# A softmax over rows of 512: one load for the first tile, two blocks in the first tile, and a third row of five tiles scaled on ScalarE

## The chip, the cores and the metric

The kernel runs on one core of a Trainium2 chip. The metric is the device time of an execution in microseconds (us), here the median of several executions. The profile's clock starts a little later and ends a little earlier: the profiled execution of the kernel before took 162.04 us, its span is 160.3 us, and its last store landed at 159.4 on the span's clock. So I add 2.6 to 2.8 us to a landing to compare it with a time. A transfer is issued by an engine and carried by 16 DMA engines; it has landed when the last of the 16 reports its part done.

## The reference

```python
batch, seq, dim = 16, 1024, 512              # x is float32
x_scaled = x / 0.5
x_max = np.max(x_scaled, axis=-1, keepdims=True)
exp_x = np.exp(x_scaled - x_max)
return exp_x / np.sum(exp_x, axis=-1, keepdims=True)
```

That is 16,384 rows of 512: 33.55 MB in and 33.55 MB out.

## The kernel before

The rows are cut into 8 tiles of 128 partitions x 16 rows x 512, 4.19 MB each. A tile goes through these steps, in place: a load, issued by SyncE; the rows' maxima on VectorE (`shift`); the exponentials and their sums on ScalarE; the reciprocal and the scaling of most rows on VectorE; the scaling of the last rows on ScalarE; a store, issued by ScalarE. Six tiles are held at once in SBUF, the memory of the core (`BUFS = 6`), so the loads of tiles 0 to 5 are issued at once, and those of tiles 6 and 7 wait until the stores of tiles 0 and 1 have landed. A tile may be computed in blocks of rows; the first and the last are.

```python
    WHOLE = [(0, G)]                                            # G = 16
    LOADS = [[(0, 4), (4, G)]] + [WHOLE] * 7
    BLOCKS = [[(0, 4), (4, 8), (8, G)]] + [WHOLE] * 6 + [[(0, 8), (8, G)]]
    STORES = [WHOLE] * 8
    BUFS = 6
    # ... (cut: pools, a warm-up of the exponential, load(), shift(), exponentials())
    def scale_vector(i):
        c, lo, hi = blocks[i]
        b = hi - lo
        k = b - b // 8                                          # 14 of 16 rows, 7 of 8
        recips[i] = stats.tile([P, BMAX], fp32, name="recip")
        nc.vector.reciprocal(recips[i][:, 0:b], sums[i][:, 0:b])
        rows = chunks[c][:, lo : lo + k, :]
        nc.vector.tensor_mul(
            rows, rows, recips[i][:, 0:k].unsqueeze(2).broadcast_to((P, k, D))
        )

    def scale_scalar(i):
        c, lo, hi = blocks[i]
        b = hi - lo
        for g in range(b - b // 8, b):
            row = chunks[c][:, lo + g, :]
            nc.scalar.activation(
                out=row, in_=row, func=COPY, scale=recips[i][:, g : g + 1]
            )
    # ... (cut: store(), issued by ScalarE)
    for i in range(n):
        if i + 1 < n:
            exponentials(i + 1, rows(i + 1)[0])
        scale_vector(i)
        scale_scalar(i)
        if i + 2 < n:
            shift(i + 2)
        store(i)
        # ... (cut)
```

## Time and profile before

162.24 us, the median of 3 executions (162.10 to 162.29).

| what | value | where |
|---|---|---|
| VectorE busy | 134.6 us, 84% of the span | busy times |
| ScalarE busy | 102.2 us, 64% | busy times |
| 16 DMA engines busy | 97.9% | the two DMA queues, summed |
| rate of the DMA engines, stores alone | 434 GB/s | windows, 116 to 147.5 us |
| last store issued, landed | 147.5, 159.4 us | ScalarE's timeline, DMA issues |

A busy share tells how full an engine is, not whether the end hangs on it. Two of these resources are nearly full. The profile's chain of waits follows instructions back from the last one, and a transfer that is issued and then only has to finish is not in it.

### The profile page before, as it was taken

The numbers are of one execution on the slowest core, as the hardware profiler recorded it, in microseconds if no ns is written. First come the engines' busy times: TensorE is split into PE (matmuls) and PEld (weight loads), VectorE is DVE, ScalarE is ACT, GpSimd is POOL, SyncE is SP. The second block draws the span as 40 slices with busy tenths as digits, with TensorE's granted clock in tenths as the row PEclk, the third lists the DMA queues.
The fourth block names the chain that finished last, engine by engine and source line by source line (L and its number), as shares of the span: only waits on it lengthen the run. The fifth ranks groups of instructions, "written<-read, shape, count | busy, mean of one in ns | idle before, by whom it ended". The sixth has DMA issues, their size and how long they took to land.

```text
span 160.3 us, 402 instructions
## 1 busy us (share of the span) xinstructions
DVE 134.6 (84%) x45; ACT 102.2 (64%) x273; POOL 0.2 (0%) x4
## 2 busy tenths in 40 slices
DVE  0607999999999999999999999999999999957000
ACT  3071549069989972998199909991899891690000
POOL 0000000000000000000000000000000000000000
DMA  5999999999999999999999999999999999999993
GB/s 180 474 409 491 409 401 483 425 393 452 458 393 401 393 425 474 409 393 499 417 393 474 442 393 468 442 393 442 474 393 417 491 401 401 491 417 401 466 442 139
DMA packets 2450, 67.13 MB, mean 419 GB/s; under 512 B 272, under 2 KB 272, under 8 KB 272
## 3 DMA queue, kind: packets, MB, share of 16 engines
q1 hardware_dynamic: 1296, 33.56, 49.4%
q10 hardware_dynamic: 1152, 33.55, 48.5%
q14 instruction: 2, 0.02, 0.0%
HBM read 33.55 MB, written 33.55 MB: 419 GB/s over the span
## 4 chain that ended last, share of the span: by engine, by line
DVE 80%; DMA 7%; ACT 4%; issue 0%; SPq 0%
DVE negmax L74 42%; DVE xt L103 36%; DMA xt<-in_x_dram 7%; ACT xt L86 4%; DVE bias L78 1%; DVE recip L101 1%; SPq L66 0%
## 5 line engine op out<-in xcount | busy, mean ns | idle before, releaser
L86 ACT ACTIVATE xt<-xt,bias 128x512 f32<-128x512 f32 x128 | 90.4, 708 | 41.5 <-DVE bias L78 40.6
L74 DVE TENSOR_REDUCE negmax<-xt 128x16 f32<-128x8192 f32 (+2 forms) x11 | 69.9, 6353 | 9.5 <-DMA xt<-in_x_dram 9.5
L103 DVE TENSOR_TENSOR xt<-xt,recip 128x7168 f32<-128x7168 f32 (+2 forms) x11 | 62.0, 5637 | 0.4
L86 ACT ACTIVATION_READ_ACCUMULATOR xt<-xt,bias 128x1 f32 x128 | 23.9, 187 | 0.0
L112 ACT ACTIVATE xt<-xt,recip 128x512 f32<-128x512 f32 x15 | 9.9, 707 | 0.0
L101 DVE RECIPROCAL recip<-sums 128x16 f32<-128x16 f32 (+2 forms) x11 | 2.4, 218 | 1.8 <-ACT xt L86 1.8
L78 DVE TENSOR_SCALAR bias<-negmax 128x16 f32<-128x16 f32 (+2 forms) x11 | 1.9, 173 | 0.4
L52 ACT ACT_TABLE_LOAD x1 | 1.3, 1283 | 0.7 <-PEq L157 0.7
L51 DVE MEMSET warm<- 128x1 f32 x1 | 0.1, 59 | 0.8 <-PEq L157 0.8
L52 ACT ACTIVATE warm<-warm 128x1 f32<-128x1 f32 x1 | 0.2, 202 | 0.0
L157 POOL MEMSET const-bfloat16-1.0<- 128x1 bf16 x1 | 0.1, 101 | 0.0
L157 POOL MEMSET const-uint8-127<- 128x1 uint8 x1 | 0.1, 101 | 0.0
L157 POOL MEMSET const-float32-0.0<- 128x1 f32 x1 | 0.1, 98 | 0.2 <-issue 0.2
L157 POOL MEMSET const-float32-1.0<- 128x1 f32 x1 | 0.1, 98 | 0.0
## 6 DMA issues: line engine op xcount, KB each, us to landing
out_dram<-xt ACTq DMA_DIRECT2D x8, 4096.0 KB, 22.8
xt<-in_x_dram SPq DMA_DIRECT2D x7, 4096.0 KB, 30.1
xt<-in_x_dram SPq DMA_DIRECT2D x1, 3072.0 KB, 11.7
xt<-in_x_dram SPq DMA_DIRECT2D x1, 1024.0 KB, 4.8
```

What stands on the lines that cost most here:

```text
L51: nc.vector.memset(warm, 0.0)
L52: nc.scalar.activation(out=warm, in_=warm, func=EXP)
L74: nc.vector.tensor_reduce(negmax[:, 0:b], chunks[c][:, lo:hi, :], axis=AX, op=MAX, negate=True)
L78: nc.vector.tensor_scalar_mul(biases[i][:, 0:b], negmax[:, 0:b], 2.0)
L86: nc.scalar.activation(out=row, in_=row, func=EXP, bias=biases[i][:, g : g + 1], scale=2.0, accum_out=sums[i][:, g : g + 1],)
L101: nc.vector.reciprocal(recips[i][:, 0:b], sums[i][:, 0:b])
L103: nc.vector.tensor_mul(rows, rows, recips[i][:, 0:k].unsqueeze(2).broadcast_to((P, k, D)))
L112: nc.scalar.activation(out=row, in_=row, func=COPY, scale=recips[i][:, g : g + 1])
L157: nc = _bacc.Bacc("TRN2", target_bir_lowering=False, num_devices=1)
```

## The change

Its intent: fewer and larger transfers and instructions at the start, and 2.7 us of scaling moved from VectorE, the fuller of the two engines that compute, to ScalarE.

```diff
-    LOADS = [[(0, 4), (4, G)]] + [WHOLE] * 7
-    BLOCKS = [[(0, 4), (4, 8), (8, G)]] + [WHOLE] * 6 + [[(0, 8), (8, G)]]
+    LOADS = [WHOLE] * 8
+    HALVES = [(0, 8), (8, G)]
+    BLOCKS = [HALVES] + [WHOLE] * 6 + [HALVES]
...
+    def vector_rows(i):
+        c, lo, hi = blocks[i]
+        if hi - lo < G:
+            return hi - lo - 1
+        return G - 3 if 1 < c < C - 1 else G - 2
...
-        k = b - b // 8
+        k = vector_rows(i)
...
-        for g in range(b - b // 8, b):
+        for g in range(vector_rows(i), b):
```

## The prediction

> **What bounds the kernel now.** I read the page first, its busy shares and its DMA rows, because the kernel moves 67 MB and does little with it.
>
> ```profile
> DVE 134.6 (84%) x45; ACT 102.2 (64%) x273; POOL 0.2 (0%) x4
> DMA  5999999999999999999999999999999999999993
> GB/s 180 474 409 491 409 401 483 425 393 452 458 393 401 393 425 474 409 393 499 417 393 474 442 393 468 442 393 442 474 393 417 491 401 401 491 417 401 466 442 139
> q1 hardware_dynamic: 1296, 33.56, 49.4%
> q10 hardware_dynamic: 1152, 33.55, 48.5%
> DVE 80%; DMA 7%; ACT 4%; issue 0%; SPq 0%
> ```
>
> VectorE is busy for 84% of the span, but the 16 DMA engines for 49.4 + 48.5 = 97.9%: the loads (q1) and the stores (q10) fill every slice but the first and the last. The chain of waits gives 80% to VectorE all the same. That is not a contradiction: the chain is followed back from the last instruction, not from the last byte, and the last store, issued by an instruction that counts as idle, is not in it. Two resources are nearly full at once, so the question is which one the end hangs on. The windows view over stages of my choosing says it.
>
> ```profile
> 2.00:13.00 11.00, 2.63 (x3) 3.13 (x10) 0.00 (x0) 1.00 1.00 420
> 13.00:45.00 32.00, 31.79 (x13) 19.73 (x54) 0.00 (x0) 1.00 1.02 439
> 45.00:69.00 24.00, 23.86 (x8) 19.72 (x55) 0.00 (x0) 1.00 1.01 421
> 69.00:116.00 47.00, 46.79 (x13) 34.98 (x95) 0.00 (x0) 1.00 1.00 432
> 116.00:147.50 31.50, 29.46 (x11) 23.37 (x62) 0.00 (x0) 1.00 1.00 434
> ```
>
> The columns are the stretch, its length, busy us (count) of VectorE, ScalarE and GpSimd, the clock, the DMA share and GB/s. From 2 us on the DMA share is 1.0 in every stage, whether loads run alone (2 to 45), both run, or stores alone (116 to 147.5). VectorE has nothing to do for most of 2 to 13, and the DMA rate is the same there.
>
> The end, from the timelines of VectorE and ScalarE and from the DMA view cut to the instant at which each of the last stores is issued:
>
> ```profile
> 143.53 3.89 DVE L103 TENSOR_TENSOR xt<-xt,recip 128x3584 f32<-128x3584 f32 x1
> 133.03 0.34 ACTq L120 DMA_DIRECT2D out_dram<-xt  x1
> 147.50 0.34 ACTq L120 DMA_DIRECT2D out_dram<-xt  x1
> ...
> out_dram<-xt ACTq DMA_DIRECT2D x1, 4096.0 KB, 16.7
> ...
> out_dram<-xt ACTq DMA_DIRECT2D x1, 4096.0 KB, 11.9
> ```
>
> The store of tile 6 is issued at 133.03 and lands 16.7 later, at 149.7. That of tile 7 is issued at 147.5, when VectorE is done, and lands 11.9 later, at 159.4. The two landings are 9.7 us apart; 4.19 MB at 434 GB/s take 9.66 us. So the last store followed the one before without a gap: it stood in a queue. How long? The first load is issued at 0.73 and the first two microseconds carried 49 GB/s x 2 us = 0.1 MB, 0.23 us at the full rate, so bytes flow some 1.0 us after an issue. The store of tile 7 could have started at 148.5; its place came at 159.4 - 9.7 = 149.7, less some tenths between last byte and landing. **The end hangs on bytes; the last store has a slack of about 0.8 us.** This slack is the number that matters: VectorE work taken away before it brings nothing, and VectorE work added costs only what exceeds it.
>
> **What the Trainium skill says.** "DMA: Bandwidth & Descriptors", section Specifications, gives a fabric ceiling of 435 GB/s for the core's 16 engines; the trace agrees, with 434 GB/s where stores run alone. The same page, section Issuing engines are not separate DMA queues, says that transfers issued by different engines end on the same 16 DMA engines and interleave; the trace agrees: with both queues live the rate stays at 421 to 432, so the queues divide one budget. "VectorE: DVE Perf Modes" says a tensor_tensor on fp32 stays in the 1x mode at 0.96 GHz (section on the 2x_2P mode): 512 / 0.96 = 533 ns a row, and the trace's (7.626 - 3.892) / 7 rows = 533 ns agrees. "ScalarE: Activation LUTs", section What ACT_TABLE_LOAD costs, says that back-to-back ACTIVATEs overlap by about 93 ns; the trace has two scaling copies in 1.32 us although one takes 0.707, so a further copy costs about 0.62 us.
>
> **The change, part by part.**
>
> *Load of tile 0 as one transfer.* The two loads landed at 1.15 + 11.65 = 12.8 us together; one load of the same bytes should land at 12.5 to 12.8. What goes is the early start: before, VectorE reduced rows 0 to 3 at 5.55 and ScalarE did their exponentials, inside a stretch in which both then idled until 12.8. Bytes unchanged: one transfer less of 17.
>
> *Tile 0 in two blocks of 8.* Replay of VectorE from 12.8, durations from the groups by form: reduce 8 rows until 17.26 and its bias; reduce the other 8 until 21.78. It then waits for ScalarE, which starts at 17.47 and needs 5.78 for eight rows (as in 137.51 to 143.29): 23.25. Scale 7 rows (pitch 3.81 with its reciprocal 0.24) until 27.30; reduce tile 1 (8.72) until 36.02; reciprocal and second block's scale: tile 2's reduction starts at 40.14. Before it started at 37.41: **VectorE is 2.7 us later**, 1.5 of it the new wait for ScalarE, the rest work that used to be done before 12.8.
>
> *Third row to ScalarE in tiles 2 to 6.* Each VectorE scale falls from 14 to 13 rows: 5 x 0.533 = **2.7 us earlier**. The two cancel: the second half of tile 7 is reduced at 132.86 + 2.73 - 2.67 = 132.9, and the store of tile 7 issued at about 147.6, against 147.5. The tail itself has the same blocks as before. ScalarE pays 5 x 0.62 = 3.1 us, a cycle of 11.3 + 1.9 + 0.4 = 13.6 against VectorE's 16.62 - 0.53 = 16.1: its idle time per tile falls from about 4.0 us ("ACT waits for DVE bias") to about 2.9, and it stays off the path.
>
> *Store issues.* Before at 44.1, 59.0, 75.6, 92.2, 108.8, 125.5, 133.0, 147.5. My replay has 46.9, 61.7, 78.9, 94.9, 111.0, 127.3, 135.3, 147.6: later by the shift that is left and by the third copy ahead of the issue. Do the DMA engines run dry? The loads of six tiles are queued at the start and last, alone, until about 12.5 + 5 x 9.7 = 61 us, so the first store still meets a full load queue. Where only stores are left, landings stand 9.7 apart back from 159.4: stores 4, 5 and 6 land at 130.3, 140.0, 149.7, each behind its predecessor. Store 5 must be issued before 130 - 1, store 6 before 139, store 7 before 148.5; the replay meets each by 1.7, 3.7 and 0.9 us. Load 6 waits for store 0, now landing some 2 us later, but by then store 1 (61.7) is queued and fills the engines, and load 7 in turn lands long before its tile's reduction.
>
> **Sum:** no byte removed, no gap opened or closed: 0 us. One transfer less, and a slightly shorter stretch in which loads and stores mix (421 to 432 against 434 to 439 GB/s apart; some 5 us less of it at 2% is 0.1), could give 0.1 to 0.3. From 162.24 I take **162.0 us**.
>
> **The rivals.** (1) *VectorE is the bound*, as the chain of waits suggests. Then the net of +2.7 and -2.7 decides, also about 0; but were the late start wholly hidden in the wait for the load, the end would come 2.7 us earlier, near 159.5. Against it: landings exactly a transfer apart. (2) *The late start isn't recovered*: ScalarE becomes the pacer with its third copy, or the first store's delay lets the DMA engines idle. If all 2.7 us came through, less 0.8 of slack, 164.1. For it: stores are issued after the copies on ScalarE's queue, and the margins of store 5 and 7 are under 2 us. Against it: ScalarE's idle of 2.9 us per tile. (3) *Whole loads move faster*: the first 1 MB took 4.8 us, more than the 2.4 that its bytes need, but that is a start-up that the single load pays too. It would give at most a few tenths.
>
> **Range and chances.** The runs of before spread over 0.2 us. The byte bound gives a floor of about 161.5; a missed margin gives up to 163. I take 161.6 to 162.6 for 8 in 10. A change by 2% is 3.2 us: faster would need bytes to vanish or a rate above any seen here; slower needs the whole late start unrecovered, and more. Faster 0.01, same 0.98, slower 0.01.
>
> **What would show it.** In the changed profile: DMA share 1.0 in the same stages and about 98% in all; the reduction of tile 2 starting near 40.1 and the last half tile's near 132.9; a new wait of VectorE for ScalarE of about 1.5 us before the first reciprocal; ScalarE's wait for the bias lower by about 1 us per tile from tile 2 on; the last store issued near 147.6 and landing near 159.3. I am wrong if a slice in mid-span falls under 9, if the last store's issue-to-landing falls to 10.7 us or so (then it found no queue, and compute sets the end), or if the last landing isn't 9.7 after the one before.

## The result, and the profile after

162.46 us (162.03 to 162.57, 6 executions) against 162.22 us for the kernel before (162.10 to 162.38, 6 executions). The ratio is 1.0009, with a 95% interval of 0.9996 to 1.0022: no difference that these runs can tell from none. Ratios here and below are the mean time of one kernel's fast runs over that of the other's of the same rounds, so not quite the ratio of the medians that stand beside them.

The page of the changed kernel: busy times, the DMA row in 40 slices, the two DMA queues, the chain of waits.

```profile
DVE 131.0 (82%) x41; ACT 105.7 (66%) x279; POOL 0.2 (0%) x4
DMA  7999999999999999999999999999999999999993
q1 hardware_dynamic: 1152, 33.55, 49.4%
q10 hardware_dynamic: 1152, 33.55, 48.4%
DVE 76%; DMA 8%; ACT 7%; issue 0%
```

VectorE lost 3.6 us of work (134.6 to 131.0) and the span did not shrink. The DMA engines are as full as before, 97.8%.

Its windows, over the same stretches as the prediction's: stretch, length, busy us of VectorE, ScalarE and GpSimd, clock, DMA share, GB/s. The view counts a packet of a transfer (32 KB as a rule) whole in the window in which it starts, so a share can exceed 1.00, and short windows are coarse.

```profile
2.00:13.00 11.00, 0.13 (x1) 0.21 (x2) 0.00 (x0) 1.00 0.91 390
13.00:45.00 32.00, 30.55 (x11) 20.72 (x58) 0.00 (x0) 1.00 1.01 434
45.00:69.00 24.00, 23.86 (x8) 19.26 (x52) 0.00 (x0) 1.00 1.01 419
69.00:116.00 47.00, 46.79 (x13) 38.42 (x102) 0.00 (x0) 1.00 1.00 432
116.00:147.50 31.50, 29.55 (x11) 25.77 (x68) 0.00 (x0) 1.00 1.00 433
```

The first row shows what was taken away: between 2 and 13 us both engines now do nothing, where before they did 2.63 and 3.13 us of work. From 13 us on the rates are those of before, within about 1%.

From VectorE's timeline: the first reciprocal, which waits for ScalarE; the reduction of tile 2; that of the last half tile.

```profile
23.31 0.20 DVE L108 RECIPROCAL recip<-sums 128x8 f32<-128x8 f32 x1 [1.29 <-ACT xt L87]
...
40.19 8.68 DVE L75 TENSOR_REDUCE negmax<-xt 128x16 f32<-128x8192 f32 x1
...
132.97 4.41 DVE L75 TENSOR_REDUCE negmax<-xt 128x8 f32<-128x4096 f32 x1
```

From ScalarE's timeline, the issue of the last two stores, and from the DMA issues at these moments their times to landing:

```profile
135.30 0.34 ACTq L127 DMA_DIRECT2D out_dram<-xt  x1
147.61 0.34 ACTq L127 DMA_DIRECT2D out_dram<-xt  x1
```

```profile
out_dram<-xt ACTq DMA_DIRECT2D x1, 4096.0 KB, 14.7
...
out_dram<-xt ACTq DMA_DIRECT2D x1, 4096.0 KB, 12.1
```

At tile 2 VectorE is 2.8 us behind the kernel before (40.19 against 37.41), at the last half tile 0.1 (132.97 against 132.86). The loss at the start is given back, 0.53 us a tile, by the third row. The store before the last lands at 135.3 + 14.7 = 150.0, the last at 147.6 + 12.1 = 159.7: 9.7 us apart, as before.

### The profile page after: what moved, and what is told of

Its sections match the earlier page's. It is cut to its first block, busy times and chain, and to the rows that moved or that the text cites. A ratio compares the mean times of both kernels' runs of the same rounds, so it can differ in the third digit from the quotient of the medians.

```text
span 160.5 us, 402 instructions
## 1 busy us (share of the span) xinstructions
DVE 131.0 (82%) x41; ACT 105.7 (66%) x279; POOL 0.2 (0%) x4
## 4 chain that ended last, share of the span: by engine, by line
DVE 76%; DMA 8%; ACT 7%; issue 0%
DVE negmax L75 40%; DVE xt L110 34%; DMA xt<-in_x_dram 8%; ACT xt L87 7%; DVE bias L79 1%; DVE recip L108 1%
## 5 line engine op out<-in xcount | busy, mean ns | idle before, releaser
L75 DVE TENSOR_REDUCE negmax<-xt 128x16 f32<-128x8192 f32 (+1 forms) x10 | 69.7, 6973 | 12.0 <-DMA xt<-in_x_dram 12.0
L110 DVE TENSOR_TENSOR xt<-xt,recip 128x6656 f32<-128x6656 f32 (+2 forms) x10 | 58.7, 5866 | 0.3
L119 ACT ACTIVATE xt<-xt,recip 128x512 f32<-128x512 f32 x21 | 13.7, 705 | 0.0
L108 DVE RECIPROCAL recip<-sums 128x16 f32<-128x16 f32 (+1 forms) x10 | 2.3, 227 | 3.1 <-ACT xt L87 3.1
L79 DVE TENSOR_SCALAR bias<-negmax 128x16 f32<-128x16 f32 (+1 forms) x10 | 1.7, 173 | 0.3
```

The costliest lines, as they stand in the source:

```text
L75: nc.vector.tensor_reduce(negmax[:, 0:b], chunks[c][:, lo:hi, :], axis=AX, op=MAX, negate=True)
L79: nc.vector.tensor_scalar_mul(biases[i][:, 0:b], negmax[:, 0:b], 2.0)
L110: nc.vector.tensor_mul(rows, rows, recips[i][:, 0:k].unsqueeze(2).broadcast_to((P, k, D)))
L119: nc.scalar.activation(out=row, in_=row, func=COPY, scale=recips[i][:, g : g + 1])
```

## The experiments

The theory has two parts. The bytes set the end: the DMA engines never run dry, and the last store stands in their queue. And the queue is short: a last store that comes more than 0.8 to 1.0 us later than in the kernel before finds idle engines, and from there compute sets the end. The main rival is that VectorE sets it, as the chain of waits suggests, so that the change gives nothing only because +2.7 and -2.7 cancel.

### The third row alone

The kernel before, with only this:

```diff
-        k = b - b // 8
+        k = vector_rows(i)        # 13 in tiles 2 to 6, else as before; ScalarE the rest
```

> The kernel before with only the third ScalarE row in tiles 2 to 6. VectorE does 5 x 0.533 = 2.7 us less, nothing else changes. Theory (bytes set the end; the last store stands in a queue): the last store is issued near 144.8 instead of 147.5, lands near 159.4 as before, so its issue to landing grows from 11.9 to about 14.6 us, and the time stays at 162.2 (within 0.3). Rival (VectorE, which the chain of waits shows, sets the end): 159.5.

Measured: 162.25 us against 162.28; ratio 1.0003 (0.9990 to 1.0016). The chain of waits of this kernel, the issue of its last store and that store's time to landing:

```profile
DVE 78%; DMA 7%; ACT 4%; issue 0%; SPq 0%
```

```profile
144.70 0.34 ACTq L127 DMA_DIRECT2D out_dram<-xt  x1
```

```profile
out_dram<-xt ACTq DMA_DIRECT2D x1, 4096.0 KB, 14.9
```

VectorE is done 2.8 us earlier than before (144.7 against 147.5) and the store takes 3.0 us longer (14.9 against 11.9). It lands at 159.6, within 0.2 us of where it landed before. All that compute gained became time in the queue. The chain still gives 78% to VectorE: here it is simply the wrong place to look. The rival's 159.5 us is excluded.

### The start alone

The changed kernel without its third row:

```diff
-        return G - 3 if 1 < c < C - 1 else G - 2
+        return G - 2
```

> The changed kernel without its third ScalarE row: the whole first load and the two blocks alone. VectorE is 2.7 us later than in either kernel, the last store issued near 150.3. Theory: with no queue left the last store takes about 11.05 us from issue to landing (1.0 to the first bytes, 9.7 for the bytes, 0.36 to the landing), so it lands near 161.3 and the time is about 164.0, 1.8 over the kernel before: the shift less a slack of 0.9. Rival (VectorE sets the end): the whole shift, 164.9 to 165.1. Rival (the DMA engines hide it all): 162.2.

Measured: 164.15 us against 162.28; ratio 1.0116 (1.0102 to 1.0129), so 1.9 us slower. The window before the last store gets going, the store's issue, and its time to landing:

```profile
148.50:151.50 3.00, 1.92 (x1) 0.00 (x0) 0.00 (x0) 1.00 0.43 186
```

```profile
150.50 0.34 ACTq L127 DMA_DIRECT2D out_dram<-xt  x1
```

```profile
out_dram<-xt ACTq DMA_DIRECT2D x1, 4096.0 KB, 11.1
```

Now the DMA share falls to 0.43 while VectorE finishes, and the store takes 11.1 us, the time of a 4.19 MB store that meets no queue. It was issued 3.0 us later than in the kernel before, and 1.9 of them came through.

With the third row and the start each alone, the four kernels form a square (the changed kernel was timed in other rounds, beside 162.22 for the kernel before):

| us | start as before | start changed |
|---|---|---|
| two rows on ScalarE | 162.28 | 164.15 |
| three rows on ScalarE | 162.25 | 162.46 |

The third row is worth 0.0 in one column and 1.7 in the other. A part of a change has no worth of its own where two bounds are this close. The two blocks without the whole load were not run.

### The whole load alone

The kernel before, its blocks of 4, 4 and 8 kept:

```diff
-    LOADS = [[(0, 4), (4, G)]] + [WHOLE] * 7
+    LOADS = [WHOLE] * 8
```

> The kernel before with its first tile loaded by one transfer, its blocks of 4, 4 and 8 rows kept. By a replay VectorE is some 3.1 us later from tile 1's reduction on (24.6 becomes 27.7), the last store issued near 150.6. Theory: 3.1 less a slack of 0.9, 164.4. Rival (VectorE sets the end): 165.3. If instead the single transfer lands earlier or the engines move whole loads faster, less than 164.

Measured: 164.88 us (164.44 to 165.85); ratio 1.0167 (1.0141 to 1.0194). The fastest executions are where the theory has them, the slower ones are not, and the median lies between the theory and the rival. The profiled execution was one of the slower (165.35). A window shortly before its last store starts, and that store's issue and landing:

```profile
149.00:151.50 2.50, 1.73 (x1) 0.00 (x0) 0.00 (x0) 1.00 0.12 52
```

```profile
150.81 0.34 ACTq L120 DMA_DIRECT2D out_dram<-xt  x1
```

```profile
out_dram<-xt ACTq DMA_DIRECT2D x1, 4096.0 KB, 11.9
```

The share of 0.12 is that of 2 engines in 16. Fourteen had run dry and waited for the last store, as the theory says; two were behind with earlier stores. A transfer lands when its slowest engine is done, so this store took 11.9 us although most engines met no queue: by the trace's landing records 14 engines had landed by 161.90, 11.1 us after the issue, the other two at 162.34 and 162.75. In the store before it the two were 2.7 and 3.1 us behind the rest (152.67 and 153.08 against 149.98), so even here the last two landings stand 9.7 us apart. The theory's part of the loss is there; the rest is stragglers. What makes an engine fall behind was not found.

### The slack, measured

The kernel before, with 15 rows on VectorE in two tiles:

```diff
-        k = b - b // 8
+        k = vector_rows(i)        # 15 in tiles 2 and 3, else as before; ScalarE the rest
```

> The kernel before with one ScalarE row instead of two in tiles 2 and 3: VectorE 2 x 0.533 = 1.07 us later at its end, last store issued near 148.6. This measures the slack. Theory: slack 0.9, so 0.2 remains: 162.3 to 162.5, and issue to landing falls to 11.1 or so. Rival (VectorE sets the end): 163.3.

Measured: 162.42 us against 162.28; ratio 1.0007 (0.9993 to 1.0021). The last store:

```profile
148.63 0.34 ACTq L127 DMA_DIRECT2D out_dram<-xt  x1
```

```profile
out_dram<-xt ACTq DMA_DIRECT2D x1, 4096.0 KB, 11.1
```

It is issued 1.1 us later and the time is not measurably longer; its 11.1 us say that the slack is just used up. The slack of the kernel before is therefore about 11.9 - 11.1 = 0.8 us in its profiled execution, which was 0.2 us faster than the median. By the median times it is 1.0 to 1.1: here 1.1 us of delay cost 0.1, and in the start alone 3.0 cost 1.9. It is the slack of the slowest engine: in the kernel before 15 engines had landed by 158.89 and the last at 159.41.

### Fewer bytes

A direct test of the bound: one row of sixteen of tiles 0 to 5 is never stored. First in the kernel before, then in the kernel with the third row alone, which has queue to spare.

```diff
-                    out=outr[c][:, lo:hi, :], in_=chunks[c][:, lo:hi, :]
+                    out=outr[c][:, lo:cut, :], in_=chunks[c][:, lo:cut, :]   # cut = 15 for c < 6
```

> Wrong result on purpose: the kernel before with the same 1.57 MB left out of its stores. Its last store is issued at 147.5 whatever the bytes. Theory (two bounds 0.9 us apart): only the slack of 0.9 comes off before the issue of the last store sets the end, 161.2 to 161.5, and its issue to landing falls from 11.9 to about 11.05. Rival (bytes alone): 158.6. Rival (bytes don't matter): 162.2.

> Wrong result on purpose: the kernel before with the third ScalarE row, whose stores of tiles 0 to 5 leave out one row of sixteen, 6 x 0.262 = 1.57 MB or 3.6 us at 434 GB/s; compute is as before. Last store issued near 144.7. Theory (bytes set the end, with 3.9 us of queue to spare): nearly all of the 3.6 us comes off, 158.5 to 159.0. Rival (VectorE, or a fixed cost elsewhere, sets the end): 162.2.

Measured: the kernel before with fewer bytes takes 161.23 us against 162.29 (ratio 0.9930, 0.9910 to 0.9950), the one with the third row 159.36 us (ratio 0.9827, 0.9795 to 0.9860). Both results are wrong. The first, its windows before the last store and that store:

```profile
143.00:146.50 3.50, 3.14 (x2) 1.52 (x4) 0.00 (x0) 1.00 0.61 262
146.50:148.50 2.00, 0.96 (x1) 0.00 (x0) 0.00 (x0) 1.00 0.53 229
```

```profile
out_dram<-xt ACTq DMA_DIRECT2D x1, 4096.0 KB, 11.1
```

Same compute, 3.6 us fewer bytes, and 1.1 us come off: then the engines run dry from about 145 us on and the issue of the last store sets the end. With the third row as well, 2.9 us come off. I expected 158.5 to 159.0 there. Its trace, taken in the slowest of its executions (160.26), shows what held it: VectorE's wait for the load of tile 7, the issue of the last store, and its time to landing.

```profile
119.02 4.42 DVE L74 TENSOR_REDUCE negmax<-xt 128x8 f32<-128x4096 f32 x1 [0.54 <-DMA xt<-in_x_dram]
...
145.50 0.34 ACTq L128 DMA_DIRECT2D out_dram<-xt  x1
```

```profile
out_dram<-xt ACTq DMA_DIRECT2D x1, 4096.0 KB, 12.1
```

The store was issued 0.8 us later than I had put it, and 15 engines had landed by 156.61, 11.1 us after the issue; one came at 157.62. So the queue ran out here too, and compute set the end again, with one late engine on top in this execution. Each bound holds the other's gain back, and they stand about 1 us apart.

### Loads and stores in one queue

The prediction had put a rate of 421 GB/s around 45 to 69 us down to loads and stores running together. If that cost were real, taking turns should be faster. The changed kernel, with the stores issued by SyncE on the loads' queue; and the same with tile 7 stored in halves:

```diff
-                nc.scalar.dma_start(
+                nc.sync.dma_start(
                     out=outr[c][:, lo:hi, :], in_=chunks[c][:, lo:hi, :]
                 )
+                if c in (1, 2):
+                    load(c + 5)
...
+    for c in range(BUFS):
+        load(c)
     shift(0)
...                                       # the second kernel only:
-    STORES = [WHOLE] * 8
+    STORES = [WHOLE] * 7 + [HALVES]
```

> The changed kernel with its stores issued by SyncE, on the queue of the loads, in the order loads 0 to 5, stores 0 and 1, load 6, store 2, load 7, stores 3 to 7: transfers follow one another instead of loads and stores sharing the engines. An estimate from the traces: while both queues are live a tile takes about 9.87 us of the engines, alone 9.68; in some 60 to 66 us of mixing that is about 1.2 us lost. Theory: the queue of the last store shrinks by about 1.2 us, of which only the slack of about 1.0 can be taken, so the time is about 161.3 to 161.6. Rival (mixing costs nothing, the rate is one budget however divided): 162.2 to 162.5. Rival (a single queue has a gap at each turn from load to store): above 162.5.

> As the one-queue kernel, with tile 7 stored in two halves, the first when its block is done near 141.6, so that the last store has only half the bytes (4.85 us) and compute no longer bounds the end. Theory: all of the about 1.2 us saved by not mixing shows, 161.0 to 161.2; if the one-queue kernel is already at 161.0 this adds nothing. Rival (mixing costs nothing): 162.2 to 162.5.

Measured: 164.07 us (162.63 to 164.74) and 163.78 us (162.66 to 164.36), against 162.22. Both ratios are 1.0092. My expectation was wrong. First the stretch around the first store, in the kernel before, in the changed one and in this one-queue kernel; then the end of the one-queue kernel.

```profile
46.50:49.50 3.00, 3.00 (x1) 3.00 (x9) 0.00 (x0) 1.00 0.98 339
```

```profile
49.50:52.50 3.00, 3.00 (x1) 3.00 (x9) 0.00 (x0) 1.00 1.07 350
```

```profile
57.00:61.50 4.50, 4.50 (x2) 4.50 (x14) 0.00 (x0) 1.00 0.99 350
61.50:66.00 4.50, 4.47 (x3) 0.49 (x2) 0.00 (x0) 1.00 1.01 437
...
158.00:159.00 1.00, 0.00 (x0) 0.00 (x0) 0.00 (x0) 1.00 0.08 33
159.00:160.00 1.00, 0.00 (x0) 0.00 (x0) 0.00 (x0) 1.00 0.08 33
```

The low rate is not spread over the mixed stretch. It is one dip of 3 to 4.5 us around the first store, with the engines busy and moving less, and it is there with one queue as with two; it moves with the first store. At the end, one engine in 16 (0.08 of the share) still works when the others are done: again a straggler, 2.1 us behind the other 15 (161.51 against 159.43) where in the kernel before it was 0.5. Mixing as such costs nothing that these traces show.

The single packets in these three traces say it more sharply. Outside the dip, 98 to 99% of the packets of 32 KB take 1.20 to 1.23 us, loads and stores alike, alone or mixed. In the dip some 25 take 1.3 to 2.1 us, about 0.8 us lost by each engine, and all of them are packets of loads, the last before the first store's own begin; the store's own take 1.21 from the first, where it has a queue of its own. And in the one-queue kernel at least 15.7 of the 16 engines are busy in every quarter of a microsecond from 13 to 145 us: the rival of a gap at each turn from load to store, whose number (above 162.5) the time met, is not what happened.

### A first store before the rest

Can the dip be paid early, while nothing else runs? A tiny store at the start, overwritten later, once in the kernel with the third row and once in the changed kernel:

```diff
+    nc.scalar.dma_start(out=outr[0][:, 0, 0:1], in_=warm)
     nc.scalar.activation(out=warm, in_=warm, func=EXP)
```

> The kernel before with the third ScalarE row (last store issued near 144.7, so some 4 us of queue to spare) and one more, tiny store (512 bytes of zeros into the rows of tile 0's output, written over later) issued by ScalarE at the start. In all traces so far the engines move 339 to 350 GB/s instead of 420 to 440 for some 3 us around the first store, about 0.8 us lost by each of the 16 engines, on one queue as on two; this asks whether it is a cost of the first store as such. Theory (a first-store cost that can be paid while nothing else runs): the dip vanishes, the engines finish 0.8 us earlier, 161.4 to 161.6. Rival (a cost of the first large store, or not avoidable): the dip stays, 162.2 to 162.5.

> The changed kernel with the same tiny first store. Its last store is issued near 147.6 with a slack of about 1.0 us. Theory: the 0.8 us fit in the slack, so 161.5 to 161.8, and the last store's issue to landing falls from 12.05 to about 11.2. Rival (dip not avoidable): 162.3 to 162.6.

Measured: 162.97 us (ratio 1.0054, 1.0038 to 1.0069) and 164.90 us (ratio 1.0177, 1.0156 to 1.0198). In the first of them the dip is where it was:

```profile
46.50:49.50 3.00, 2.96 (x3) 2.92 (x9) 0.00 (x0) 1.00 0.96 317
```

So the dip goes with the turn to the first large store, not with the first store as such, and 512 bytes do not buy it off; its cause was not found. Where the added time went the traces do show: the 16 engines landed the last store between 158.42 and 159.95 in the first kernel and between 158.75 and 161.83 in the second, against 158.44 to 159.41 in the kernel before. It is stragglers again; why there are more of them was not settled. No correct version tried beats the kernel before.

## Why the prediction was right

**What bounds the kernel.** Right, and now shown: taking 2.8 us from VectorE gave 0.0 us, taking 3.6 us of bytes gave 1.1 us with VectorE as before and 2.9 where VectorE had 2.7 us less to do.

**The slack of about 0.8 us.** Right, for the profiled execution and its slowest engine: 11.9 us in the kernel before against 11.1 in each of the three kernels (the start alone, the slack run, fewer bytes) where the last store meets no queue.

**The start.** Predicted: the reduction of tile 2 at 40.14, and a wait of 1.5 us for ScalarE. Measured: 40.19 and 1.29; the whole load landed at 0.73 + 12.12 = 12.85 us. Alone this part cost 1.9 us, the shift less the slack.

**The third row.** Predicted: the last half tile's reduction at 132.9, ScalarE's idle time per tile from 4.0 to 2.9 us. Measured: 132.97, and 2.86. ScalarE did not become the pacer.

**The issues of the stores.** Predicted 46.9, 61.7, 78.9, 94.9, 111.0, 127.3, 135.3 and 147.6. The changed kernel's ScalarE issued them at 46.90, 61.76, 78.99, 95.08, 111.16, 127.25, 135.30 and 147.61. No gap opened.

**The rivals.** VectorE as the bound fell with the third row alone. The late start that is not recovered is exactly what the run without the third row shows: the prediction gave it 164.1, the run 164.15. The agreement to 0.05 is luck: the prediction took 2.7 us less a slack of 0.8, the run had 3.0 less 1.1. Whole loads did not move faster: the single load landed at 12.85 us, the two of before at 12.80.

**What was off.** The few tenths that I took off, for one transfer less and a shorter mixed stretch, did not come: 162.46, not 162.0. The interval (0.9996 to 1.0022) leaves room for no difference, but not for a gain of 0.2 us (0.9985). One of its two terms rested on a wrong reading. The 421 GB/s were not a cost of mixing but an average over the dip at the first store, and that dip is in both kernels (419 GB/s in the changed one, over the same stretch). And two of the tests that I offered are not safe: the time from issue to landing, and the distance of the last two landings, tell of a queue only if no engine straggles. In the run with the whole load alone they stayed at 11.9 and 9.7 us with 14 of 16 engines dry. The 10.7 us that I gave for a store without a queue was also 0.4 too low, as it left out the time from the last byte to the landing. The floor of 161.5 has no working, and no run tests it.

## What to carry to other kernels

Before you trust a chain of waits that ends in compute, ask what the last transfer does after its issue: if its landing stands one full transfer after the one before it, at least its slowest engine was in a queue; if most of the engines were, the length of that queue is the only part of compute's time that is free. The DMA share just before it can start shows which: 1.00 up to 147.5 us in the changed kernel, 0.12 from 149 to 151.5 us in the run with the whole load alone. Compare its time with that of a transfer that meets no queue; the difference is the slack, and work moved between engines pays only outside it. When a change has parts with opposite effects, run each alone and add nothing up: here one part was worth 0.0 or 1.7 us, depending on the other.

## What the Trainium skill lacked or had wrong

- "DMA: Bandwidth & Descriptors", section Where 436 GB/s comes from, says that for transfers between HBM and SBUF the HBM side, about 358 GB/s, binds. It says so without the condition that the page itself gives further up, under Measured: 358 is what each of two cores gets when both stream. This core alone moved 432 to 434 GB/s for 78 us (69 to 147.5), close to the fabric figure of 435 of the same page; 358 did not bind here.
- The same page, section Anatomy of one DMA, fits the time of a transfer only for those issued by GpSimd: 2.0 us plus the bytes at 436 GB/s, 11.6 us for 4.19 MB. A store of that size issued by ScalarE that met no queue took 11.1 us in three runs.
- I found no page that has the dip at the first large store: 317 to 350 GB/s for 3 to 4.5 us, about 0.8 us lost by each engine on load packets just before the store's own, in every kernel looked at for it, on one queue or two, and not removed by a tiny store ahead of it.
- The same page's section on why a DMA increments its semaphore by 16 says that the engines finish independently. It has no size for how far they drift: here one engine of 16 held the end back by about 2 us (share 0.08 from 158 us on, landing at 161.5), and in another run two of 16 stood 2.7 and 3.1 us behind.
